# Eight transfers for the replicated bias rows, earlier key matrices, alternating banks and an uneven last scaling in a hybrid attention and mLSTM layer

## The chip, the cores and the metric

The kernel runs on one core of one Trainium2 chip. The time is device microseconds (us) of one execution; where several are given, the median counts. All arithmetic is float32, with most matrix products made of three products of a high and a low part.

## The reference, cut to what matters

One layer: a combined input projection, attention over three dilated windows with a shared relative position bias, an mLSTM branch beside it, gates, one output projection and two RMS norms.

```python
xn = rmsnorm(h, norm_in_g[layer])
proj = xn @ w_in[layer]                       # 512 x 1024 times 1024 x 12288
q_a, k_a, v_a, z_a, x_m, z_m, o_m, gates = jnp.split(proj, SPLIT_POINTS, axis=-1)
y_a = dilated_attention(to_heads(q_a), to_heads(k_a), to_heads(v_a), rel_bias)   # 16 heads of 64
y_a = (y_a * jax.nn.silu(z_a)) @ w_pa[layer]
y_m = mlstm_branch(x_m, z_m, o_m, ...) @ w_pb[layer]                             # 4 heads of 512
g_a, g_m = jnp.split(jax.nn.sigmoid(gates + gate_b[layer]), 2, axis=-1)
h = h + (g_a * y_a + g_m * y_m) @ w_out[layer]
return rmsnorm(h, norm_out_g)

# in dilated_band_attention
bias = rel_bias[t5_bucket(jnp.clip(delta, 0, band) * dilation)]
logits = jnp.where(valid, logits + bias, -jnp.inf)
```

## The kernel before

The stages are, in the order of the code: the first projections of the mLSTM input (`xm`), convolution, folded key products (`kp`) and score matrices (`S`) for 16 column tiles `ct`, four to an mLSTM head; then the four heads (`head(h)`), each with its output gate `om` (made by `proj_n`), its numerators `num`, its gate `zm` (made by `pair_t` from pairs of weight chunks), transposes `hT`, the values of the next head (`block_v`, tile `v`, from four reloaded key tiles `xmr`), the next head's output gate, and the projection `ym`; then eight pairs of attention heads (`qa`, `ka`, `za`, `sa`, `pT`, `pv`; the values `va` for four pairs at a time, made by `proj_n` too); then the gates, `ya`, and the output rows `out` in four tiles of 128 rows.

**Weights.** `weights` or `pair_weights` fetches a 128x1024 chunk (512 KB) into one of five buffers `raw`; ScalarE rounds it to a high part `whi` and VectorE subtracts to make the low part `wlo`. All loads are issued by SyncE (SP) on one queue; only the very last half row goes by ScalarE's queue.

**The bias.** `rel_rows` makes 16 rows `frow` of 640 values, one for each attention head, writes them to a scratch tensor `fd`, and replicates each 128 times into the scratch tensor `fr` (16 x 128 x 640) by one transfer from `fd`, whose source repeats a row with a stride of zero. Each attention head later loads its skewed tile `tb` from `fr`. `rel_rows` is called right after `head(0)`.

**The order.** Nothing runs in the order of the code. `Recorder` notes every operation, and `issue` lays them out on the engines with costs and delays of its own before anything is built; each engine's instructions then stand in that fixed order. An engine that is free takes the operation with the smallest `prio` among those that are ready and whose buffers have room. `prio` is the operation's number in the code less `R.ahead`; a weight chunk has 300 ahead (`AHEAD`). A load waits for no data, so all loads of the rest of the kernel stand in SP's list from early on, held back by their buffers alone. The search of that list ends here:

```python
while ready[e]:
    x = heapq.heappop(ready[e])
    if room(x[2]):
        op = x[2]
        break
    blocked.append(x)
    if len(blocked) > 40:
        break
```

So an operation behind more than 40 that have no room is not seen. A transfer costs SP 60 ns in the plan and takes, on one link for all, its output's elements times 4 bytes at 359 bytes a nanosecond; it waits there for earlier transfers. The plan knows nothing of the 16 DMA engines. In the code, one pair of attention heads is 206 operations.

**PSUM.** There are two banks of the kind `mm` and six of the kind `x` (`sc_bank`). `proj_n` makes its four row tiles in `mm` banks, in turn with `ym` and two of `pair_t`'s three products.

**The end.** For each of the four row tiles, `rsqrt1` gives the factor `z`, and the row is scaled in two halves: columns 0 to 511 by ScalarE, 512 to 1023 by VectorE, each followed by its store.

Of the kernel before, what the change touches and what calls it, by code (L numbers as in the profile page):

```python
# [14 lines left out]
AF = mybir.ActivationFunctionType  # L15
OP = mybir.AluOpType

P = 128
T = 512
NT = T // P  # L20
D = 1024
# [3 lines left out]
HEADS_A = 16  # L25
# [312 lines left out]
def hybrid_layer(ctx, tc, a, out):  # L338
    nc = tc.nc
    R = Recorder(nc, a["win"].tensor)  # L340
    V, A, PE, G, SP = (R.engine(e) for e in ("vector", "scalar", "tensor", "gpsimd", "sync"))
# [8 lines left out]
    def tile_of(pool, shape, dt, name, tag, cap, psum=False):  # L350
        return R.buf(lambda: pool.tile(shape, dt, name=name, tag=tag, bufs=cap), shape, dt, tag, cap, psum)

    def slot(name, dt=F32):
        return tile_of(upool, [P, 516], dt, name, "u", NSLOT)

    def mm_bank(name):
        return tile_of(psum, [P, 512], F32, name, "mm", 2, True)

    def sc_bank(name):
        return tile_of(psum, [P, 512], F32, name, "x", 6, True)  # L360
# [18 lines left out]
    def dram(name, shape):  # L379
        return R.buf(lambda: dpool.tile(shape, F32, name=name), shape, F32, dram=True)  # L380
# [42 lines left out]
    def weights(src):  # L423
        R.ahead = AHEAD
        hl = halves(fetch(src))
        R.ahead = 0
        return hl
# [217 lines left out]
    def proj_t(chunk, name, x=None):  # L645
        hl = weights(a["win"][chunk])
        ps = mm_bank(name)
        for k in range(NK):
            proj_k(ps, hl, x or list(zip(xh, xl)), k)
        return ps  # L650

    def proj_n(chunk, name):
        hl = [weights(a["win"][chunk + c]) for c in range(4)]
        for t in range(NT):
            ps = mm_bank(name)
            tt = slice(t * P, (t + 1) * P)
            for k in range(NK):
                hi, lo = hl[k // 2]
                c = slice((k % 2) * T, (k % 2 + 1) * T)
                mm3(ps, xh[k][:, tt], xl[k][:, tt], hi[:, c], lo[:, c], k == 0, k == NK - 1)  # L660
            yield ps
# [72 lines left out]
    def fold_qk(h):  # L734
        m = spread(mrow, h, "M")
        Mh, Ml = slot("Mh", F32R)[:, :512], slot("Ml", F32R)[:, :512]
        sc = 512.0 ** -0.5
        A.activation(Mh, m, AF.Copy, scale=sc)
        V.scalar_tensor_tensor(Ml, m, sc, Mh.bitcast(F32), op0=OP.mult, op1=OP.subtract)
        return Mh, Ml  # L740
# [30 lines left out]
    for ct in range(NMT):  # L771
        h, c = divmod(ct, 4)
        for e in range(max(EARLY, ct + LEAD) if ct else EARLY, min(ct + LEAD + 1, NMT)):
            raw_x = e < UNNORMED
            ps = proj_t(CXM + e, "xm", xu if raw_x else None)
            R.ahead = EMPTY
            m_of.append(x_m(e, ps, rb if raw_x else None))
            R.ahead = 0
        if FIRST <= ct < FIRST + NK // 2:
            normalise(2 * (ct - FIRST))  # L780
            normalise(2 * (ct - FIRST) + 1)
        if c == 0:
            Mh, Ml = fold_qk(h)
            sps = [sc_bank("S") for _ in range(3)]
        m = m_of[ct]
        if ct == 8:
            block_v(0)
        xc = conv_silu(m, ct)
        ch, cl = split(xc, "xc")
        s = slot("sx")[:, :T]  # L790
        A.activation(s, xc, AF.Copy, scale=hs[:, 16 + ct:17 + ct])
        SP.dma_start(sxd[ct], s)
        ps = sc_bank("kp")
        cc = slice(c * P, (c + 1) * P)
        mm3(ps, Mh[:, cc], Ml[:, cc], ch, cl, True, True)
        kh, kl = split(ps[:, :T - P], "kp", T - P)
        kf = slot("kf")[:, :P]
        A.activation(kf, ps[:, T - P:], AF.Copy)
        if ct == 0:
            fold_gates()  # L800
        waiting.append((ct, m, xc))
        if c == 3:

            R.together()
            for ct_, m_, xc_ in waiting:
                for i, (w, x) in enumerate(((1, m_[:, 3:259]), (1, m_[:, 259:515]), (0, xc_[:, :256]), (0, xc_[:, 256:]))):
                    PE.matmul(gps[32 * i:32 * i + 32, :256], ust[w][:, ct_, :], x, start=ct_ == 0, stop=ct_ == NMT - 1,
                              tile_position=(0, 32 * i))
            R.apart()
            waiting = []  # L810
        for j in range(NT - 1):
            t0 = j * P
            ss = slice(t0, t0 + P)
            mm3(sps[j][:, :T - t0], kh[:, ss], kl[:, ss], ch[:, t0:], cl[:, t0:], c == 0, c == 3 and j < 2)
        PE.matmul(sps[2][:, 256:384], kf, xc[:, T - P:], start=False, stop=c == 3)
        if c == 3:
            sr = wide("sraw")
            A.activation(sr[:, 0:512], sps[0], AF.Copy)
            A.activation(sr[:, 512:896], sps[1][:, :384], AF.Copy)
            A.activation(sr[:, 896:1280], sps[2][:, :384], AF.Copy)  # L820
            SP.dma_start(srd[h], sr)
        if ct == 11:
            R.ahead = -400
            tx = quarters()
            R.ahead = 0
# [6 lines left out]
    ps = sc_bank("gsum")[:36]  # L832
# [23 lines left out]
    ps = sc_bank("aT")  # L856
    for t in range(NT):
        tt = slice(t * P, (t + 1) * P)
# [136 lines left out]
    def rel_rows():  # L995
        onehot = raw_chunk("onehot", 64)[:, :640]
        SP.dma_start(onehot, a["onehot"])
        relb = const("relb", [32, HEADS_A], F32)
        SP.dma_start(relb, a["rel_bias"])
        ohr, rel2 = wide("ohr", F32R)[:64, :640], const("rel2", [64, HEADS_A], F32R)  # L1000
        A.activation(ohr, onehot, AF.Copy)
        A.activation(rel2[:32], relb, AF.Copy)
        V.tensor_sub(rel2[32:], relb, rel2[:32].bitcast(F32))
        lnm = raw_chunk("lnm", 16)[:, :640]
        SP.dma_start(lnm, a["lnmask"])
        frow = raw_chunk("frow", 16)[:, :640]
        for c0 in (0, 320):
            ps = sc_bank("frow")[:16, :320]
            PE.matmul(ps, rel2, ohr[:, c0:c0 + 320], start=True, stop=True)
            V.tensor_add(frow[:, c0:c0 + 320], ps, lnm[:, c0:c0 + 320])  # L1010
        fd = dram("fd", [16, 640])
        SP.dma_start(fd, frow)
        fr = dram("fr", [16, P, 640])
        SP.dma_start(fr, fd[:, None, :].to_broadcast([16, P, 640]))
        return fr

    vals = []

# [15 lines left out]
    for h in range(HEADS_M):  # L1034
        head(h)
        if h == 0:
            fr = rel_rows()


    yaf = []  # L1040
    for p in range(HEADS_A // 2):
        if p % 4 == 0 and p:
            vals.append(values(p))
        vv = vals[-1]
        qps = proj_t(CQ + p, "qa")
        qh = [slot("qh", F32R)[:, :T] for _ in range(2)]
        ql = [slot("ql", F32R)[:, :T] for _ in range(2)]
        for w in range(2):
# [4 lines left out]
                                   op0=OP.mult, op1=OP.subtract)  # L1053
# [9 lines left out]
        z = silu2(proj_t(CZA + p, "za"), "za")  # L1063
        ya = slot("ya")[:, :T]
        tmp = slot("yt")[:, :T]
        for w in range(2):
# [6 lines left out]
            for i in range(NT):  # L1073
                n = P * (i + 1)
                N = max(n, 256)
                ps = sc_bank("sa")
# [14 lines left out]
            for j in range(NT):  # L1091
                t0 = j * P
                q0 = min(t0, T - 256)
                ps = sc_bank("pT")
# [36 lines left out]
    for d in range(NK):  # L1131
        hi, lo = weights(a["wpa"][d])
        ps = mm_bank("ya")
# [26 lines left out]
    for t in range(NT):  # L1160
        tt = slice(t * P, (t + 1) * P)
        xr, og = raw_chunk("xr"), raw_chunk("og")
        SP.dma_start(xr, a["x"][tt, :])
        w = T if t < NT - 1 else T // 2
        n = D // w
        ss = [small("so", 1) for _ in range(n)]
        for i in range(n):
            cc = slice(w * i, w * i + w)
            ps = mm_bank("out")[:, :w]
            c, o = divmod(w * i, T)  # L1170
            for d in range(NK):
                mm3(ps, mh[d][:, tt], ml[d][:, tt], woh[d][c][:, o:o + w], wol[d][c][:, o:o + w], d == 0, d == NK - 1)
            V.scalar_tensor_tensor(xr[:, cc], ps, 0.5, xr[:, cc], op0=OP.mult, op1=OP.add)
            junk = slot("junk")[:, :w]
            A.activation(junk, xr[:, cc], AF.Square, accum_out=ss[i])
            if 0 < i < n - 1:
                V.tensor_add(ss[i], ss[i], ss[i - 1])
            V.scalar_tensor_tensor(og[:, cc], xr[:, cc], -0.5 * D ** 0.5, go[:, cc], op0=OP.mult, op1=OP.mult)
        v = small("vo", 1)
        V.tensor_scalar(v, ss[n - 1], ss[n - 2], D * EPS, op0=OP.add, op1=OP.add)  # L1180
        z = rsqrt1(v, "ro")
        A.activation(xr[:, :T], og[:, :T], AF.Copy, scale=z)
        (A if t == NT - 1 else SP).dma_start(out[tt, :T], xr[:, :T])
        V.tensor_scalar(xr[:, T:], og[:, T:], z, None, op0=OP.mult)
        SP.dma_start(out[tt, T:], xr[:, T:])

    with tc.manual_schedule():
        R.run([{"u": k, "mm": 0, "x": 2, "small": 8} for k in (0, 4, 8, 16, 64)])
# [7 lines left out]
EMPTY = 300  # L1196
# [92 lines left out]
```

## Time and profile before

| what | value |
|---|---|
| median of 3 runs | 886.04 us (885.03 to 887.89) |
| the profiled execution | 883.73 us |
| its span, first to last instruction | 881.8 us |
| TensorE matmul (PE) busy | 863.8 us, 98% of the span |
| VectorE (DVE) busy | 661.8 us, 75% |
| ScalarE (ACT) busy | 471.2 us, 53% |
| mean granted TensorE clock | 0.996 |
| chain that ended last, by engine | PE 89%, DMA 6%, DVE 2%, ACT 1% |

The profile is of one execution. PE busy counts matmuls whose ends are modelled, so small gaps between them don't show. Nearly every operation goes through the recorder and carries its line, L333; operations are told apart by their tiles. "SPq" is the issuing of a transfer by SyncE, and an x and a number behind a row count merged instructions. "Granted clock" is the share of TensorE's full speed that the throttle allowed.

### The profile page before, as it was taken

Reading aid. Unit: us, or ns where it says so; the run is one execution under the profiler, and the core shown is the slowest. Engines: PE = TensorE matmul, PEld = TensorE weight load, DVE = VectorE, ACT = ScalarE, POOL = GpSimd, SP = SyncE. Lnnn points to the kernel's source line nnn. Section 1 sums busy time; section 2 is a strip of 40 time slices with the busy share of each in tenths; the row PEclk is TensorE's granted clock in tenths of the full one; section 3 lists DMA queues with packets and bytes.
Section 4 is the critical chain, followed back from the end, with each engine's and each line's share of the span. In section 5 each row is a group of like instructions: output and inputs, shape, how many; then the busy total and the mean of one; then the engine's idle time right before and its main releaser. Section 6 shows DMA issues by size and latency. Waiting matters only on the chain.

```text
span 881.8 us, 13364 instructions
## 1 busy us (share of the span) xinstructions
PE 863.8 (98%) x4916; PEld 741.7 (84%) x4916; DVE 661.8 (75%) x1361; ACT 471.2 (53%) x879; POOL 10.9 (1%) x70
## 2 busy tenths in 40 slices
PE   7999999999998999999999999999999999999997
PEld 6778877798888889988988888888888899998886
DVE  4899889799557867967865487874778899888533
ACT  7668876655323522551333477654667665674222
POOL 0000000000000000000000000000000000000000
PEclk9999999999999999999999999999999999999999
DMA  9834443234339422511424322212222123356021
GB/s 317 318 132 161 162 166 116 89 123 150 102 121 335 149 72 96 199 61 52 159 81 144 120 82 87 97 60 96 83 77 80 61 73 119 119 170 214 25 72 48
DMA packets 39962, 110.00 MB, mean 125 GB/s; under 512 B 4436, under 2 KB 6228, under 8 KB 39896
## 3 DMA queue, kind: packets, MB, share of 16 engines
q1 hardware_dynamic: 39752, 108.87, 36.0%
q8 instruction: 39, 0.64, 0.3%
q10 hardware_dynamic: 144, 0.26, 0.1%
q14 instruction: 27, 0.22, 0.1%
HBM read 95.97 MB, written 18.39 MB: 130 GB/s over the span
## 4 chain that ended last, share of the span: by engine, by line
PE 89%; DMA 6%; DVE 2%; ACT 1%; SPq 1%; issue 0%; POOL 0%; ACTq 0%
PE ym L333 10%; PE om L333 10%; PE gate L333 9%; PE zm L333 7%; PE xm L333 7%; PE out L333 5%; PE va L333 5%; PE ya L333 5%; PE qa L333 5%; PE za L333 5%; PE ka L333 4%; DMA raw<-in_win_dram 4%; PE S L333 3%; PE num L333 2%; PE sa L333 2%; PE pv L333 2%
## 5 line engine op out<-in xcount | busy, mean ns | idle before, releaser
L333 DVE TENSOR_TENSOR wlo<-raw,whi 128x1024 fp32r<-128x1024 f32 (+1 forms) x126 | 146.9, 1170 | 81.4 <-ACT whi L333 81.0
L333 ACT ACTIVATE whi<-raw 128x1024 fp32r<-128x1024 f32 (+1 forms) x126 | 127.8, 1017 | 145.6 <-PE ym L333 44.8
L333 ACT ACTIVATE whi<-s 128x512 fp32r<-128x512 f32 (+1 forms) x32 | 26.9, 841 | 51.1 <-PE ym L333 11.9
L333 PE MATMUL om<-whi,xh 128*128 128x512 f32 x128 | 51.1, 399 | 0.0
L333 PE MATMUL om<-whi,xl 128*128 128x512 f32 x128 | 50.7, 396 | 0.0
L333 PE MATMUL ym<-yh,whi 128*128 128x512 f32 x128 | 50.7, 396 | 0.0
L333 PE MATMUL om<-wlo,xh 128*128 128x512 f32 x128 | 50.6, 395 | 0.0
L333 PE MATMUL ym<-yl,whi 128*128 128x512 f32 x128 | 50.5, 395 | 0.0
L333 PE MATMUL ym<-yh,wlo 128*128 128x512 f32 x128 | 50.4, 394 | 0.0
L333 ACT ACTIVATE p<-p,mx 128x128 f32<-128x128 f32 (+1 forms) x64 | 35.6, 558 | 14.5 <-DVE mx L333 14.2
L333 DVE CUSTOM_DVE_ANT_0 p<-sa,tb 128x128 f32<-128x128 f32 (+1 forms) x64 | 28.8, 484 | 14.4 <-PE sa L333 14.4
L333 PE MATMUL zm<-th,whi 128*128 128x256 f32 x128 | 36.9, 288 | 0.0
L333 PE MATMUL zm<-tl,whi 128*128 128x256 f32 x128 | 36.5, 285 | 0.0
L333 PE MATMUL zm<-th,wlo 128*128 128x256 f32 x128 | 36.5, 286 | 0.0
L333 PE MATMUL gate<-th,wlo 128*128 128x256 f32 x128 | 36.3, 284 | 0.0
L333 PE MATMUL gate<-tl,whi 128*128 128x256 f32 x128 | 36.1, 282 | 0.0
L333 PE MATMUL gate<-th,whi 128*128 128x256 f32 x128 | 35.9, 282 | 0.0
L333 DVE SCALAR_TENSOR_TENSOR conv<-xm,half,conv 128x512 f32<-128x512 f32 x48 | 35.4, 745 | 0.3
L333 PE MATMUL xm<-xl,whi 128*128 128x512 f32 x88 | 35.3, 401 | 0.0
L333 DVE TENSOR_TENSOR ymacc<-ymacc,ym 128x512 f32<-128x512 f32 x24 | 16.5, 686 | 24.8 <-PE ym L333 24.8
L333 PE MATMUL xm<-xh,wlo 128*128 128x512 f32 x88 | 34.8, 397 | 0.0
L333 PE MATMUL xm<-xh,whi 128*128 128x512 f32 x88 | 34.6, 395 | 0.0
(294 smaller groups left out, 2682.1 us busy)
## 6 DMA issues: line engine op xcount, KB each, us to landing
raw<-in_win_dram SPq DMA_DIRECT2D x94, 512.0 KB, 3.5
raw<-in_wpb_dram SPq DMA_DIRECT2D x16, 512.0 KB, 4.3
fr<-fd SPq DMA_DIRECT2D x1, 5120.0 KB, 21.8
xmd<-xm SPq DMA_DIRECT2D x16, 256.0 KB, 2.2
sxd<-sx SPq DMA_DIRECT2D x16, 256.0 KB, 2.0
xmr<-xmd SPq DMA_DIRECT2D x16, 256.0 KB, 4.8
sxr<-sxd SPq DMA_DIRECT2D x16, 256.0 KB, 4.8
tb<-fr SPq DMA_DIRECT2D x16, 256.0 KB, 3.6
```

Source lines behind the costliest of these rows:

```text
L333: getattr(getattr(self.nc, op.eng), fn)(*a, **k)
```

## The change

The transfer into `fr` becomes eight, each for two heads (a pair). The first is recorded where the one stood, after `head(0)`; the transfer for pair p + 1 is recorded at the start of pair p. `fold_qk` (three operations for each mLSTM head: `M` on VectorE, `Mh` on ScalarE, `Ml` on VectorE) gets 300 ahead. In `proj_n`, row tiles 1 and 3 take an `x` bank in place of an `mm` bank. In the last scaling ScalarE takes 384 columns and VectorE 640.

```diff
@@ def proj_n(chunk, name):
-            ps = mm_bank(name)
+            ps = (mm_bank, sc_bank)[t % 2](name)
@@ for ct in range(NMT):
         if c == 0:
+            R.ahead = EMPTY
             Mh, Ml = fold_qk(h)
+            R.ahead = 0
             sps = [sc_bank("S") for _ in range(3)]
@@ def rel_rows():
         fd = dram("fd", [16, 640])
         SP.dma_start(fd, frow)
-        fr = dram("fr", [16, P, 640])
-        SP.dma_start(fr, fd[:, None, :].to_broadcast([16, P, 640]))
-        return fr
+        return fd, dram("fr", [16, P, 640])
+
+    def rel_spread(p):
+
+        hh = slice(2 * p, 2 * p + 2)
+        SP.dma_start(fr[hh], fd[hh, None, :].to_broadcast([2, P, 640]))
@@ for h in range(HEADS_M):
         head(h)
         if h == 0:
-            fr = rel_rows()
+            fd, fr = rel_rows()
+            rel_spread(0)
@@ for p in range(HEADS_A // 2):
         if p % 4 == 0 and p:
             vals.append(values(p))
         vv = vals[-1]
+        if p + 1 < HEADS_A // 2:
+            rel_spread(p + 1)
         qps = proj_t(CQ + p, "qa")
@@ the last scaling
-        A.activation(xr[:, :T], og[:, :T], AF.Copy, scale=z)
-        (A if t == NT - 1 else SP).dma_start(out[tt, :T], xr[:, :T])
-        V.tensor_scalar(xr[:, T:], og[:, T:], z, None, op0=OP.mult)
-        SP.dma_start(out[tt, T:], xr[:, T:])
+        e = slice(0, 384), slice(384, D)
+        A.activation(xr[:, e[0]], og[:, e[0]], AF.Copy, scale=z)
+        (A if t == NT - 1 else SP).dma_start(out[tt, e[0]], xr[:, e[0]])
+        V.tensor_scalar(xr[:, e[1]], og[:, e[1]], z, None, op0=OP.mult)
+        SP.dma_start(out[tt, e[1]], xr[:, e[1]])
```

## Rows read from the trace of the kernel before

**Rows 1.** Waits of PE: total us, times, longest us.

```profile
PE zm L333 <- DVE p L333: 3.5, 1, 3.5
PE kp L333 <- ACT Mh L333: 1.1, 1, 1.1
```

**Rows 2.** Windows: start:end, length, busy PE, PEld, DVE, ACT, POOL; clock, DMA share, GB/s.

```profile
270.00:280.00 10.00, 10.00 (x87) 10.00 (x86) 9.73 (x22) 6.11 (x9) 0.00 (x0) 1.00 1.01 331
280.00:284.00 4.00, 2.65 (x21) 2.16 (x19) 0.24 (x1) 0.57 (x1) 0.00 (x0) 1.00 0.90 310
284.00:288.00 4.00, 1.86 (x12) 1.86 (x13) 3.48 (x7) 0.76 (x2) 0.00 (x0) 0.90 0.94 360
288.00:292.00 4.00, 4.00 (x21) 3.73 (x20) 3.03 (x6) 2.97 (x5) 0.00 (x0) 0.68 0.54 200
```

**Rows 3.** Timeline of ACT and of DVE at the stall: start, us, instruction, idle before.

```profile
283.43 1.06 ACT L333 ACTIVATE whi<-raw 128x1024 fp32r<-128x1024 f32 x1 [4.06 <-DMA raw<-in_win_dram]
...
284.52 1.23 DVE L333 TENSOR_TENSOR wlo<-raw,whi 128x1024 fp32r<-128x1024 f32 x1 [4.28 <-ACT whi L333]
285.67 0.42 DVE L333 TENSOR_TENSOR p<-zm,p 128x256 f32<-128x256 f32 x1
```

**Rows 4.** Timeline of SP's issues from the bias transfer on: start, us.

```profile
260.31 0.61 SPq L333 DMA_DIRECT2D fr<-fd  x1
260.97 7.33 SPq L333 DMA_DIRECT2D raw<-in_win_dram  x1
...
314.83 27.14 SPq L333 DMA_DIRECT2D raw<-in_win_dram  x4
342.14 2.48 SPq L333 DMA_DIRECT2D sxr<-sxd  x4
348.05 9.48 SPq L333 DMA_DIRECT2D raw<-in_win_dram  x3
358.40 10.29 SPq L333 DMA_DIRECT2D raw<-in_wpb_dram  x4
369.50 0.33 SPq L333 DMA_DIRECT2D raw<-in_win_dram  x1
369.88 1.85 SPq L333 DMA_DIRECT2D xmr<-xmd  x4
```

**Rows 5.** Transfers of the whole span: packets by size; issues, KB each, us to landing.

```profile
DMA packets 39962, 110.00 MB, mean 125 GB/s; under 512 B 4436, under 2 KB 6228, under 8 KB 39896
...
fr<-fd SPq DMA_DIRECT2D x1, 5120.0 KB, 21.8
...
selr<-in_sel_dram SPq DMA_DIRECT2D x1, 72.0 KB
...
gsel<-in_gsel_dram SPq DMA_DIRECT2D x1, 36.0 KB, 4.9
bif<-in_bif_dram SPq DMA_DIRECT2D x1, 0.0 KB
relb<-in_rel_bias_dram SPq DMA_DIRECT2D x1, 2.0 KB, 4.0
```

**Rows 6.** Packets and queues, 263 to 274 us, the bias transfer alone.

```profile
DMA packets 1436, 3.68 MB, mean 334 GB/s; under 512 B 0, under 2 KB 0, under 8 KB 1436
```

**Rows 7.** Packets, rate and landings, 874 to 882 us, the last two stores.

```profile
GB/s 0 0 0 0 0 0 0 0 0 0 0 0 0 0 0 0 0 0 0 0 0 0 0 0 236 348 440 359 389 399 358 92 0 0 0 0 0 0 0 0
DMA packets 288, 0.52 MB, mean 66 GB/s; under 512 B 32, under 2 KB 32, under 8 KB 288
...
out_dram<-xr SPq DMA_DIRECT2D x1, 256.0 KB, 2.0
```

**Rows 8.** Chain that ended last, 360 to 400 us: start, us, what.

```profile
376.81 1.78 PE v L333 x16
```

**Rows 9.** Timeline of DVE and of ACT at the end.

```profile
877.52 0.48 DVE L333 TENSOR_SCALAR xr<-og,ro_z 128x512 f32<-128x512 f32 x1
...
877.58 0.72 ACT L333 ACTIVATE xr<-og,ro_z 128x512 f32<-128x512 f32 x1 [0.74 <-DVE ro_z L333]
```

## Prediction before the result

> **What bounds the kernel now.** First the page's shares: PE is busy for 98% of the span and makes 89% of the chain that ended last, so the change can gain only where PE waits, and can lose wherever it makes PE wait. Next the waits of PE: seven rows in all, and two of them touch the change [rows 1]. The 3.5 us wait is the stall to look at; the 1.1 us one is the key matrix of the first mLSTM head. No row has PE waiting for a bank or for a bias tile. The windows place the stall at 281 to 286 us and show its second cost: TensorE ran at half clock, 1.2 of 2.4 GHz, for about 3.4 us after it, since the granted mean is 0.90 and then 0.68 over two windows of 4 us [rows 2]. That lost 0.10 x 4 + 0.32 x 4 = 1.7 us. Stall and clock: 5.2 us.
>
> The timelines say why. ACT stood idle 4.06 us for a weight chunk and converted it at 283.43; DVE made its low part behind that, and only then the sum `p` that PE waited for [rows 3]. The chunk belongs to a later product, but it stood ahead of `p` in the fixed order of ACT and DVE. It was issued at 260.97, right behind the bias transfer [rows 4], which took 21.8 us to land [rows 5].
>
> **The change part by part.** Sums go against the profiled execution, 883.73 us; it lies 2.3 us below the median of 886.04, and I add 2.3 at the end.
>
> *Where the eight transfers go.* All read `fd` alone, so all are ready once it lands. The plan issues whatever SP can reach, but not past more than 40 operations without room. The first keeps its place. Behind it at that moment stand, counted from the code, 51 loads of the remaining mLSTM heads and the six weight chunks of pairs 0 and 1 (206 operations a pair against 300 ahead): 57. So the second transfer goes when 17 more loads have gone, not at once. Each later one needs 5 more (three chunks, two `tb`); the fifth needs 6 (four chunks of `va` and two `tb`). That is behind load 17, 22, 27 and 33 after the first. Read off the SP rows, the rows left out hold 15 loads, so load 17 is the first chunk of 314.83, load 22 the second `sxr` of 342.14, load 27 the third chunk of 348.05, and load 33 the first of the four `xmr` of 369.88 [rows 4]. The last three come near 419, 433 and 445.
>
> *What one costs.* The whole transfer, alone on the engines, moved 1,436 packets in 11 us, so with 16 engines 16 x 11 / 1,436 = 0.123 us each [rows 6]. A head is 128 packets of 2,560 bytes: 15.7 us on one engine. At the best rate of the last stores, 440 GB/s [rows 7], a packet takes 0.093 us and a head 11.9 us. If two heads are spread over 16 engines, a transfer costs an eighth, about 2 us; if each head keeps one engine, it holds two engines for 11.9 to 15.7 us, and a chunk behind it, which has a share on every engine, lands that much later. No transfer in the trace has two heads, so I take the side from the nearest rows. The last two stores (two times 128 rows) carry 32 packets under 512 bytes, 16 each [rows 7]: each engine in use reports. The span has 4,436 small packets and its list of transfers, 33 rows, 268 issues. Small data packets are 128 (`gsel`), 32 (`relb`) and 4 (`bif`); the remaining 4,272 are 16 fewer than 268 x 16 [rows 5]. `bif` has 4 rows and `selr` 36, the only outer sizes that 16 does not divide: 4 and 12 engines are 12 and 4 reports fewer, 16 in all. So engines follow the outer size, and that is 2 here. I take two engines and 13 us, towards the quick end since two engines crowd the memory less than sixteen.
>
> The Trainium skill ("DMA: Bandwidth & Descriptors", section "Why a DMA increments its semaphore by 16 and not by 1") has the rule: the largest number up to 16 that divides the slowest dimension of both sides, on the lowest-numbered engines. The missing 16 reports agree with it; by it all eight transfers sit on the same two engines, and by the plan's own account, which knows one link, they cost nothing: 902 to 904 us by the one, 880 by the other.
>
> *The old stall.* The first transfer still holds two engines, but for 13 us: the chunk behind it lands near 260.3 + 13 + 1.6 (512 KB at 331 GB/s [rows 2]) + 1.3 for start and report (2.0 us to land less 0.7 of moving [rows 7]) = 276.2. ACT was free from 283.43 - 4.06 = 279.4 [rows 3]. So the stall goes: -5.2, with 3 us to spare; at 15.7 us it would still go, at 21.8 it would stay (0).
>
> *The new wait.* The second transfer delays the two chunks right behind it by some 13 us; the first delayed one by 18 us for 3.5 us of wait [rows 1, 5], so I take 0, bounds 0 and 3. The third is issued near 343.6 and holds its engines to 356.6; three chunks of 1.6 us follow, to 361.4, then the fourth transfer, to 374.4, four chunks and one more, to 382.4, the first `xmr` (0.8), the fifth transfer, to 396.2, and three `xmr`, to 398.6, landed near 399.9. In the profile PE started `v` from these tiles at 376.81 [rows 8], 6.9 us after the first issue. The wait is 23.1 us; the plan charges both transfers 1.8 us each (163,840 elements x 4 / 359) and may put `v` 3.7 us later: 19.4 us. If all four `xmr` get in ahead of the fifth transfer they land near 386.9 and the wait is 10.1 - 1.8 = 8.3. Below, if engines are shared after all: 0. I take 19.4, by the count. Behind `v` everything on PE waits, and a stall longer than the one of rows 1 brings half clock again: +1.7.
>
> *Later transfers.* The seventh falls between the last two chunks of `va`, and the second of them lands some 15 us late. The nearest case is the stall of rows 1 to 3, 18 us late for 5.2 us with the clock. Bounds 0 and 5.2; I take 3.
>
> *Key matrices.* The three operations can move ahead of others on ACT and DVE. Bounds 0 and the 1.1 us of rows 1; with `mrow` and the first convolution still to come before them, I take the half, -0.6. Later heads show no such wait.
>
> *Banks.* No wait for a bank: 0. What hides it is that each row tile's 24 matmuls outlast its evacuation. It costs if `x` banks run short beside `S`, `num` or `pT`; PE can then take a tile of the other kind. Bounds -0.5 and +2, by the size of the small waits.
>
> *Last scaling.* ACT ends last: 877.58 + 0.72 against 877.52 + 0.48 [rows 9]. A quarter fewer columns gives ACT at most 0.18 back, a quarter more costs DVE at most 0.12, and the bytes of the two stores are the same: 0, bounds -0.2 and +0.1.
>
> Sum: -5.2 - 0.6 + 19.4 + 1.7 + 3 = +18.3; 883.73 + 18.3 = 902.0, and with 2.3: **904 us**.
>
> **The rivals.**
>
> *The transfers are hidden (faster).* Either they use all engines, or the loads behind them have time to spare: chunks are mostly asked for long before use, and even 18 us of delay made only 3.5 us of wait once. For it: `fr` itself ran on all 16, and a stretch of the plan without the old stall may put `xmr` elsewhere. Against: the count of reports. Time: 883.73 - 5.8 + 2.3 = 880.2. It decides where a transfer holds the queue under 5 us, the lead of the `xmr` tiles.
>
> *One queue, one place (no change).* If the plan reached all eight at once, the same 5,120 KB would stand in the same place, and on 16 engines the stall would stay: 886.04 - 0.6 = 885.4. Against: 57 loads stand ahead, 17 more than the search allows.
>
> *The fifth transfer misses the `xmr` tiles (slower, less).* One load more or less before it decides. 883.73 - 5.8 + 8.3 + 1.7 + 3 + 2.3 = 893.
>
> **How the numbers follow.** From no change the runs here can tell about 0.3%, 2.7 us. Forecast with the full `xmr` wait 0.42, own range 895 to 912; the smaller wait 0.20 (886 to 897, nearly all of it slower); hidden 0.29 (879 to 883); one place or gains and losses that cancel 0.09. Slower 0.62, same 0.08, faster 0.30. The range must take in the hidden case below and the full wait above: 879 to 912, which leaves out about 0.15, half of it above, where packets take 0.123 us or later loads add up.
>
> **What the profile of the changed kernel would show.** Right: eight issues of `fr`, each 13 to 16 us to landing, at 640 KB; no PE wait for `p` near 281; a PE wait of some 20 us for `xmr` at the `v` of the last head, with half clock after it; windows with a DMA share near 0.13 in it. Wrong: landings of 3 to 5 us, which is the hidden case; eight issues in a row, which is the one place. The sum fails first if the order of the loads around 370 differs, or if the plan puts other work ahead of `v`.

## Result and profile after

The changed kernel takes 911.15 us (median of 4 runs, 910.08 to 912.05) against 886.18 us before: a ratio of 1.0281, 95% interval 1.0261 to 1.0302. It is slower by 2.8%, where 904 was forecast. The span of the profiled execution grew from 881.8 to 908.3 us.

The waits of PE come first again (total us, times, longest us). The wait for `p` of [rows 1] is gone; the one for `Mh` is what it was.

```profile
PE v L333 <- DMA xmr<-xmd: 16.1, 4, 8.1
...
PE va L333 <- ACT whi L333: 4.1, 1, 4.1
PE ym L333 <- DVE ymacc L333: 1.5, 1, 1.5
PE kp L333 <- ACT Mh L333: 1.1, 1, 1.1
...
PE va L333 <- DVE wlo L333: 0.5, 1, 0.5
```

SP's issues in the changed kernel show where the eight transfers went, to be read against [rows 4].

```profile
263.16 0.70 SPq L333 DMA_DIRECT2D fr<-fd  x1
263.92 5.01 SPq L333 DMA_DIRECT2D raw<-in_win_dram  x1
...
313.84 0.60 SPq L333 DMA_DIRECT2D fr<-fd  x1
314.86 27.03 SPq L333 DMA_DIRECT2D raw<-in_win_dram  x4
341.99 0.38 SPq L333 DMA_DIRECT2D sxr<-sxd  x1
342.42 0.60 SPq L333 DMA_DIRECT2D fr<-fd  x1
...
357.79 0.59 SPq L333 DMA_DIRECT2D fr<-fd  x1
359.20 9.09 SPq L333 DMA_DIRECT2D raw<-in_wpb_dram  x4
369.19 0.33 SPq L333 DMA_DIRECT2D raw<-in_win_dram  x1
369.56 0.44 SPq L333 DMA_DIRECT2D xmr<-xmd  x1
370.05 0.59 SPq L333 DMA_DIRECT2D fr<-fd  x1
376.13 11.57 SPq L333 DMA_DIRECT2D xmr<-xmd  x3
...
437.61 0.59 SPq L333 DMA_DIRECT2D fr<-fd  x1
...
452.00 0.59 SPq L333 DMA_DIRECT2D fr<-fd  x1
453.08 3.83 SPq L333 DMA_DIRECT2D raw<-in_win_dram  x1
...
463.49 0.77 SPq L333 DMA_DIRECT2D fr<-fd  x1
```

The fifth transfer stands behind the first of the four `xmr`, as counted. The other three `xmr` were not even issued for 6 us, and their issuing took 11.57 us in all where four took 1.85 us before [rows 4]. The windows of the changed kernel (columns as in [rows 2]) show PE meanwhile:

```profile
280.00:300.00 20.00, 19.54 (x126) 17.08 (x125) 19.64 (x37) 10.69 (x21) 0.23 (x3) 1.00 0.62 212
...
376.00:382.00 6.00, 1.42 (x7) 0.80 (x5) 2.07 (x4) 2.49 (x7) 0.10 (x1) 1.00 0.13 52
382.00:388.00 6.00, 4.82 (x15) 3.86 (x15) 2.36 (x5) 0.93 (x3) 0.20 (x2) 0.53 0.31 98
388.00:396.00 8.00, 0.21 (x1) 0.00 (x0) 0.00 (x0) 0.21 (x1) 0.00 (x0) 0.50 0.29 103
392.00:396.00 4.00, 0.00 (x0) 0.00 (x0) 0.00 (x0) 0.00 (x0) 0.00 (x0) 0.50 0.13 51
396.00:404.00 8.00, 7.71 (x39) 7.06 (x40) 4.23 (x9) 3.54 (x8) 0.30 (x3) 0.79 0.03 9
...
465.00:475.00 10.00, 5.46 (x18) 3.73 (x18) 2.92 (x5) 1.58 (x2) 0.00 (x0) 0.80 0.37 144
475.00:485.00 10.00, 10.00 (x39) 7.99 (x38) 8.30 (x15) 3.64 (x8) 0.00 (x0) 0.86 0.28 97
```

From 376 to 382 us the transfers keep 0.13 of 16 engines busy: two engines, moving 52 GB/s. Most of what they move then is not the bias transfer itself, as the packets of this stretch show:

```profile
DMA packets 89, 0.31 MB, mean 52 GB/s; under 512 B 10, under 2 KB 10, under 8 KB 89
```

The 79 packets that are not reports have 3.9 KB each; a row of the bias transfer has 2,560 bytes, a row of a weight chunk 4,096. The ten reports fit two for each of the five chunks issued between the fourth transfer and the first `xmr`. So the two engines still had these chunks' shares before them when the other fourteen were through with theirs. From 392 to 396 us, with the fifth transfer and the shares of the `xmr` behind it left, it is again two engines, at 51 GB/s. At that rate 640 KB take 655,360 / 51,000 = 12.9 us.

The page gives no landing time for the eight transfers, so the 13 to 16 us of the forecast can't be read directly. The time that half clock cost is the missing share of each window times its PE busy time: 2.3, 0.1, 1.6, 1.1 and 1.4 us by these rows; in the window from 465 PE stood still before the clock fell, so the share is better taken of the whole window there, 2.0.

### The profile page after: what moved, and what is told of

It is laid out like the page before. It is cut to its first block, busy times and chain, and to the rows that moved or that the text cites. A ratio compares the mean times of both kernels' runs of the same rounds, so it can differ in the third digit from the quotient of the medians.

```text
span 908.3 us, 13373 instructions
## 1 busy us (share of the span) xinstructions
PE 871.7 (96%) x4916; PEld 745.5 (82%) x4916; DVE 662.9 (73%) x1361; ACT 470.4 (52%) x879; POOL 9.5 (1%) x70
## 2 busy tenths in 40 slices
DMA packets 39962, 110.00 MB, mean 121 GB/s; under 512 B 4436, under 2 KB 6740, under 8 KB 39896
## 4 chain that ended last, share of the span: by engine, by line
PE 79%; DMA 10%; DVE 5%; ACT 3%; issue 1%; SPq 0%; ACTq 0%; DVEq 0%
PE gate L333 9%; PE ym L333 8%; PE xm L333 7%; PE om L333 6%; PE zm L333 5%; PE out L333 5%; PE ya L333 5%; PE qa L333 5%; PE za L333 5%; PE va L333 5%; DMA raw<-in_win_dram 5%; PE ka L333 4%; DMA xmr<-xmd 3%; PE S L333 3%; PE num L333 3%; PE sa L333 2%
## 5 line engine op out<-in xcount | busy, mean ns | idle before, releaser
L333 ACT ACTIVATE p<-p,mx 128x128 f32<-128x128 f32 (+1 forms) x64 | 35.6, 560 | 14.0 <-DVE mx L333 13.8
L333 PE MATMUL v<-Bv,xmr 128*128 128x128 f32 x128 | 19.9, 321 | 16.1 <-DMA xmr<-xmd 16.1
```

The costliest lines, as they stand in the source:

```text
L333: getattr(getattr(self.nc, op.eng), fn)(*a, **k)
```

## The experiments

The theory: two heads keep a transfer on two engines for about 13 us, and whatever SP issues behind it waits for its share on those two. Rival 1: the number of transfers, or their places in SP's order, cost the time. Rival 2: another part of the change does.

**The same order, on 16 engines (`fr16`).** The 128 copies become the outer dimension of the transfer; every engine keeps the changed kernel's instructions in the changed kernel's order.

```diff
-        SP.dma_start(fr[hh], fd[hh, None, :].to_broadcast([2, P, 640]))
+        SP.dma_start(fr[hh].rearrange("h p f -> p h f"), fd[None, hh, :].to_broadcast([P, 2, 640]))
```

> The changed kernel with the same instructions in the same order on every engine; only the form of the eight bias transfers differs: the 128 copies are the outer dimension in place of the two heads. Theory (a transfer of two heads sits on two engines): each transfer now lands in 3 to 6 us in place of about 16, PE's waits for xmr fall from 16.1 us to under 3, its wait at va goes, no half clock in between but near 215 us, and the time is 881 to 886 us. Rival 1 (eight transfers cost by their number or by where they stand in SP's order): about 911. Rival 2 (banks or key matrices cost the time): above 905.

Measured: 881.72 us, ratio to before 0.9941 (0.9926 to 0.9956). It is faster than both kernels, and 3% faster than the changed one by this line alone. Its PE waits:

```profile
...
PE v L333 <- DMA xmr<-xmd: 1.4, 1, 1.4
...
```

The one wait at `v` is that of the second head, before the first bias transfer was issued (261.79 us):

```profile
214.78 2.94 PE L333 MATMUL v<-Bv,xmr 128*128 128x128 f32 x24 [1.41 <-DMA xmr<-xmd]
```

Its SP issues around the last head's `xmr`:

```profile
365.67 0.42 SPq L333 DMA_DIRECT2D xmr<-xmd  x1
366.14 0.54 SPq L333 DMA_DIRECT2D fr<-fd  x1
366.79 2.04 SPq L333 DMA_DIRECT2D xmr<-xmd  x3
```

Its packets and issues over the span:

```profile
DMA packets 40075, 110.00 MB, mean 125 GB/s; under 512 B 4549, under 2 KB 6853, under 8 KB 40009
...
fr<-fd SPq DMA_DIRECT2D x8, 640.0 KB, 7.0
```

The same eight transfers in the same places, landing in 7.0 us, cost PE nothing at `va` and nothing at the `v` of the last head. Rival 1 falls, and rival 2 with it. The landing is a little over the 3 to 6 us expected; that each starts behind loads already in the queue would explain it, but isn't shown. The half clock near 215 us, expected here too, did not come.

**The eight transfers alone (`fr_only`).** Key matrices, banks and last scaling as before.

```diff
-            R.ahead = EMPTY
             Mh, Ml = fold_qk(h)
-            R.ahead = 0
...
-            ps = (mm_bank, sc_bank)[t % 2](name)
+            ps = mm_bank(name)
...
-        e = slice(0, 384), slice(384, D)
-        A.activation(xr[:, e[0]], og[:, e[0]], AF.Copy, scale=z)
...
-        V.tensor_scalar(xr[:, e[1]], og[:, e[1]], z, None, op0=OP.mult)
...
+        A.activation(xr[:, :T], og[:, :T], AF.Copy, scale=z)
...
+        V.tensor_scalar(xr[:, T:], og[:, T:], z, None, op0=OP.mult)
...
```

> The eight transfers alone, as changed; key matrices, banks and last scaling as before. Theory: 903 to 912 us, with transfers of about 16 us to landing and PE waiting for xmr or for weight chunks. Rival 2: 881 to 887.

Measured: 911.1 us, ratio 1.0262 (1.0243 to 1.028), the loss of the whole change. Its PE waits:

```profile
PE v L333 <- DMA xmr<-xmd: 17.7, 3, 8.1
...
PE va L333 <- ACT whi L333: 4.7, 1, 4.7
```

**The three other parts alone (`rest_only`).** One bias transfer as before.

```diff
-            rel_spread(0)
...
+        SP.dma_start(fr, fd[:, None, :].to_broadcast([16, P, 640]))
...
-        if p + 1 < HEADS_A // 2:
-            rel_spread(p + 1)
```

> The three other parts alone, with the one bias transfer of before. Theory: 884 to 889 us, the stall behind the bias transfer near 281 us as before (3 to 4 us). Rival 2: above 900.

Measured: 888.2 us, ratio 1.0007 (0.9993 to 1.0021): no difference. The stall of [rows 1] is there, 3.2 us.

**The fifth transfer later (`fr_fifth_later`).** Against the changed kernel:

```diff
+            R.ahead = -100 if p == 3 else 0
             rel_spread(p + 1)
+            R.ahead = 0
```

> The changed kernel, with the fifth transfer three loads later in SP's order, so that it stands behind all four xmr of the last head in place of behind the first. Theory: the wait at v falls from 16 us to 5 to 8, the half clock with it, and the time to 896 to 904 us. Rival 1: about 911, since number and sizes are the same.

Measured: 899.58 us, ratio 1.0146 (1.0126 to 1.0166). Its PE waits:

```profile
PE v L333 <- DMA xmr<-xmd: 7.5, 2, 5.8
...
PE va L333 <- ACT whi L333: 4.1, 1, 4.1
PE ym L333 <- DVE ymacc L333: 3.3, 2, 1.7
```

The fifth transfer came to stand four loads later, behind the other three `xmr` and one weight chunk; the last head's `v` waits only once:

```profile
367.05 8.21 SPq L333 DMA_DIRECT2D xmr<-xmd  x4
...
398.19 0.59 SPq L333 DMA_DIRECT2D fr<-fd  x1
```

```profile
380.75 4.26 PE L333 MATMUL v<-Bv,xmr 128*128 128x128 f32 x24 [5.84 <-DMA xmr<-xmd]
```

Number and sizes are those of the changed kernel; one place cost 11.6 us. The wait that is left at the last head's `v`, 5.84 us, is that behind the fourth transfer alone (the rest of the 7.5 is the second head's); the one at `va` stays.

**Four transfers of four heads (`fr4`).** The third falls behind the first `xmr`, with no other just ahead of it.

```diff
-        hh = slice(2 * p, 2 * p + 2)
-        SP.dma_start(fr[hh], fd[hh, None, :].to_broadcast([2, P, 640]))
+        hh = slice(4 * p, 4 * p + 4)
+        SP.dma_start(fr[hh], fd[hh, None, :].to_broadcast([4, P, 640]))
...
-        if p + 1 < HEADS_A // 2:
-            rel_spread(p + 1)
+        if p % 2 and p + 1 < HEADS_A // 2:
+            rel_spread((p + 1) // 2)
```

> The changed kernel with four bias transfers of four heads in place of eight of two; the third stands behind the first xmr of the last head, as the fifth did, but with no other just before it. Theory (one engine for each head, so 13 to 16 us on four engines, whatever the bytes): the wait at v is 7 to 10 us, one wait at va of 3 to 5 us stays, and the time is 896 to 903. Rival (two engines for a transfer, so twice the bytes take about 27 us): the wait at v is 18 us or more, and the time 905 or more. Rival (cost by the number of transfers): half of the loss is left, about 898, with waits spread over all four.

Measured: 896.21 us, ratio 1.0106 (1.0086 to 1.0126). Its PE waits:

```profile
PE v L333 <- DMA xmr<-xmd: 8.1, 2, 6.6
...
PE va L333 <- ACT whi L333: 2.7, 1, 2.7
...
PE va L333 <- DVE wlo L333: 0.8, 1, 0.8
```

At the last head's `v`, with the window in which nothing else runs:

```profile
384.61 4.59 PE L333 MATMUL v<-Bv,xmr 128*128 128x128 f32 x24 [6.58 <-DMA xmr<-xmd]
```

```profile
380.00:384.00 4.00, 0.00 (x0) 0.00 (x0) 0.00 (x0) 0.00 (x0) 0.00 (x0) 0.66 0.26 103
```

A share of 0.26 is four engines, and at 103 GB/s 1,280 KB take 12.7 us, as long as 640 KB on two. Twice the bytes hold the queue no longer: one transfer of four heads makes PE wait 6.58 us there (7 to 10 were expected), two of two heads in a row 5.75 + 8.08 = 13.8 us. So a transfer takes the time of one head, each head on an engine of its own. The time lies at the lower end of the 896 to 903 expected. That the loss is about 40% of the changed kernel's also fits a price by the number; it is `fr16`, with all eight, that excludes that.

**The eight transfers alone, on 16 engines (`fr16_only`).** `fr_only` with the line of `fr16`.

```diff
-        SP.dma_start(fr[hh], fd[hh, None, :].to_broadcast([2, P, 640]))
+        SP.dma_start(fr[hh].rearrange("h p f -> p h f"), fd[None, hh, :].to_broadcast([P, 2, 640]))
```

> The eight transfers alone, each with the 128 copies as its outer dimension; key matrices, banks and last scaling as before. Theory: as fast as the whole change with that form, 880 to 884 us, transfers landing in about 7 us, no wait near 281 us. If the three other parts were worth something, it would be 886 or more.

Measured: 881.18 us, ratio 0.994 (0.9924 to 0.9957), the same as `fr16`: the other parts add nothing to it.

**The key matrices alone (`mh_only`) and the banks alone (`bank_only`).**

```diff
+            R.ahead = EMPTY
             Mh, Ml = fold_qk(h)
+            R.ahead = 0
```

```diff
-            ps = mm_bank(name)
+            ps = (mm_bank, sc_bank)[t % 2](name)
```

> The key matrices' priority alone, with the one bias transfer. Predicted: 0.6 us off, from the wait at kp (1.1 us before). Rival, from the changed kernel's profile, where that wait is still 1.1 us: nothing, 0.998 to 1.002 of before.

> The alternating banks alone, with the one bias transfer. Predicted: no difference, 0.998 to 1.002. Rival: they move v ahead of its xmr tiles near 214 us, which brought half clock in the changed kernel, and cost 2 to 3 us (1.003).

Measured: 886.97 us, ratio 1.0 (0.9989 to 1.0012), and 887.43 us, ratio 1.0001 (0.9984 to 1.0018). Neither makes a difference that can be measured. The 0.6 us that the prediction gave to the key matrices is not there. ScalarE makes `Mh` when it did, first before, then with the key matrices alone (39.02 us in the changed kernel):

```profile
38.98 0.62 ACT L333 ACTIVATE Mh<-M 128x512 fp32r<-128x512 f32 x1
```

```profile
38.96 0.61 ACT L333 ACTIVATE Mh<-M 128x512 fp32r<-128x512 f32 x1
```

With the key matrices alone the wait at `kp` was 0.7 us and in the changed kernel 1.1, but `scale_only`, with the key matrices of before, had 2.4: it varies by more than that.

**One transfer, copies outermost (`fr_one_copies`).** The order of before, with one transfer of the other form.

```diff
-        SP.dma_start(fr, fd[:, None, :].to_broadcast([16, P, 640]))
+        SP.dma_start(fr.rearrange("h p f -> p h f"), fd[None, :, :].to_broadcast([P, 16, 640]))
```

> The kernel before with its one bias transfer, whose outer dimension is now the 128 copies; the order of all instructions is that of before. It asks whether the gain of the eight transfers with that form comes from the splitting or from the form. Theory (each of 16 engines still moves 128 packets): about 20 us to landing, the stall near 281 us stays at 3 to 5 us with half clock behind it, 0.997 to 1.002 of before. Rival (the form alone is quicker): no stall, 0.994.

Measured: 884.64 us, ratio 0.997 (0.9957 to 0.9982). Its profile has the stall of before, 3.6 us at `zm`, and a landing of 21.6 us (21.8 before), so the splitting, not the form, takes the stall away. The 0.3% that it gained has no place in this profile; it stays open, and so does whether that much of the 0.6% of `fr16` comes with the form.

**The last scaling alone (`scale_only`).**

```diff
-        A.activation(xr[:, :T], og[:, :T], AF.Copy, scale=z)
...
-        V.tensor_scalar(xr[:, T:], og[:, T:], z, None, op0=OP.mult)
...
+        e = slice(0, 384), slice(384, D)
+        A.activation(xr[:, e[0]], og[:, e[0]], AF.Copy, scale=z)
...
+        V.tensor_scalar(xr[:, e[1]], og[:, e[1]], z, None, op0=OP.mult)
...
```

> The last scaling at 384 and 640 columns alone. Predicted: nothing, 0.999 to 1.001; ACT's last instruction 0.1 us shorter, DVE's 0.07 us longer, the same bytes to store. Rival: the longer store ends later, by up to 0.5 us.

Measured: 887.76 us, ratio 0.9996 (0.9983 to 1.001). The last scalings in its timelines of DVE and ACT, against [rows 9]:

```profile
881.65 0.55 DVE L333 TENSOR_SCALAR xr<-og,ro_z 128x640 f32<-128x640 f32 x1
...
881.71 0.61 ACT L333 ACTIVATE xr<-og,ro_z 128x384 f32<-128x384 f32 x1 [0.74 <-DVE ro_z L333]
```

ACT's is 0.11 us shorter, DVE's 0.07 us longer, and the end doesn't notice.

## Why the prediction was right

*Where the transfers go.* All eight stand where the count put them: behind loads 17, 22, 27 and 33, and near 438, 452 and 463 in a kernel that was by then some 18 us late (419, 433 and 445 were forecast). Load 22 is now the first `sxr` and not the second, since a chunk had moved ahead of them. The search that stops behind 40 operations spreads them; nothing in the plan weighs them against `xmr`.

*Engines.* Two, by the share of 0.13, and four for the four heads of `fr4`, by 0.26. The list of transfers has 7 more than before, and the page still counts 4,436 packets under 512 bytes: eight transfers with 2 reports are the 16 of the one. `fr4` has 4,436 too, four transfers with 4 reports. `fr16` has 4,549, which is 113 more, where 7 x 16 = 112 were due. The Trainium skill's rule ("DMA: Bandwidth & Descriptors", section "Why a DMA increments its semaphore by 16 and not by 1") agrees with these counts; which engines the two are, no run here shows. That the fourth and the fifth transfer use the same two follows from 376 to 382 us: the fifth had been issued at 370.05, and yet only two engines were busy, with chunks that stood ahead of it.

*The terms.* The old stall went, as forecast: no wait for `p`, and a clock of 1.00 from 280 to 300 us (-5.2). At the last head's `v`, 19.4 us and 1.7 of clock were forecast; PE waited 5.75 us for the first `xmr` and 8.08 us for the others, by its timeline:

```profile
383.18 2.05 PE L333 MATMUL v<-Bv,xmr 128*128 128x128 f32 x8 [5.75 <-DMA xmr<-xmd]
...
396.29 3.96 PE L333 MATMUL v<-Bv,xmr 128*128 128x128 f32 x20 [8.08 <-DMA xmr<-xmd]
```

That is 13.8 us and, from the windows, 2.3 + 0.1 + 1.6 = 4.0 of clock: 17.8 for 21.1. The last `xmr` ended the wait at 396.3, 3.6 us before the 399.9 of the sum, and the plan had put work on `v` and `om` between the two waits, 5.0 us at half clock, where 3.7 were allowed for; the clock took more than one such stall had shown, since PE worked a stretch at half clock between the two waits. The step that was mis-sized most is `va`: 3 us were taken within bounds of 0 to 5.2, and it was 4.1 + 0.5 of wait and 2.0 + 1.4 of clock, 8.0. The bound was taken from the old stall, where ACT waited 4.06 us for the late chunk [rows 3] and the clock cost 1.7 us; here ACT waited twice as long, and the clock cost twice as much:

```profile
470.99 1.06 ACT L333 ACTIVATE whi<-raw 128x1024 fp32r<-128x1024 f32 x1 [8.66 <-DMA raw<-in_win_dram]
```

`ym` waited 1.5 us behind the second transfer, where 0 was taken and 3 allowed. The key matrices gave nothing (-0.6 was taken). Not foreseen is a stretch near 215 us, where the `v` of the second head waits 1.80 us for its `xmr` (the remaining 0.46 of the 16.1 is at the third head's), and the clock falls:

```profile
214.00:219.00 5.00, 4.43 (x25) 4.43 (x26) 3.31 (x6) 2.80 (x6) 0.00 (x0) 0.66 0.18 63
```

0.34 x 5 = 1.7 us. This comes 48 us before the first bias transfer is issued, so no bias transfer holds these loads up. The profile of every kernel here has this wait, 0.37 us before and 1.0 to 1.7 in the ten others, `scale_only` and `fr_one_copies` among them, whose order up to there is that of before. Only in the profile of the changed kernel did the clock fall after it; what settles that stays open. Together: -5.2 + 17.8 + 8.0 + 1.5 + 1.8 + 0.5 - 0.4 + 1.7 = 25.7 us, against 26.5 by the spans.

*The size.* The loss was forecast at 18 us and is 25, and 911.15 us lies less than 1 us inside the upper end of the range, 912. The place, the engines and the wait at the last head were right as a mechanism; the size was off by the `va` term (8.0 for 3), with `ym` and the stretch near 215 us at nothing, and the `v` term, 3.3 too large, made up for part of it. That the sum came this near is in part luck.

*The rivals.* The hidden case is what `fr16` measured, 881.72 us, where 880.2 was worked out for it: the mechanism was right, and it hung on the engines alone. The smaller wait, with the fifth transfer behind the four `xmr`, is `fr_fifth_later`: 899.58, where 893 was worked out. There `va` took 4.1 + 0.8 of wait and 1.7 of clock, 3.6 more than the 3 of the sum, and `ym` 3.3 where 0 was taken. The one place did not come about.

## What to carry to other kernels

Splitting the transfer helped here only where each piece still used all the engines (881.72 us, against 896.21 with four and 911.15 with two): look at the outer dimension of both sides, not at the bytes, and turn a replicating copy so that the copies stand outermost. A piece that sits on a few engines held up the loads behind it here, which had a share on those engines; its price is read from the loads behind it, not from its own row. A planner that counts bytes on one link cannot see this, so after such a change read SP's list: which loads with a short lead (here `xmr`, 7 us) come right behind a piece.

## What the runs showed of the hardware

The engine that issues can be held too: SP stood 5.01 us over the chunk behind the first transfer and 11.57 us over three `xmr`, where the other rows of a single issue show 0.3 to 0.8 us. `fr4` issued twice the bytes, and SP stood 4.68 us over the same chunk and 9.50 us over the same three `xmr`. It is not a matter of few engines alone: behind the one transfer of before SP stood 7.33 us over the chunk [rows 4], and in `fr16` 0.60 us. What holds it, no view here shows.

Two engines moved 52 GB/s of weight rows (376 to 382 us) and 51 GB/s of bias rows and `xmr` shares (392 to 396 us), 26 on each, and four in `fr4` 103, again 26 on each. The sixteen of before made 334 GB/s with the bias transfer alone, 21 on each [rows 6].
